# Seven-product FFN steps in another order, weight sums beside the down products, and the norm factor spread within the second product

## The chip, the core and the metric

The kernel runs on one core of one Trainium2 chip. The metric is the device time of one execution in microseconds, which holds the profiled span and about 1.8 us around it. Five engines work side by side, each through its own queue of instructions in a fixed order: TensorE (PE, matmuls), VectorE (DVE), ScalarE (ACT), GpSimd (POOL), and SyncE (SP), which here issues the DMAs.

## The reference, cut to what matters

```python
def _swiglu(h, w_up, w_down):
    a, g = jnp.split(h @ w_up, 2, axis=-1)
    return (jax.nn.silu(g) * a) @ w_down
...
x = x + 0.5 * _swiglu(_rmsnorm(x, g_ffn1), w_ffn1_up, w_ffn1_down)
x = x + mixer(_rmsnorm(x, g_mix), states)          # mLSTM and GLA side by side
x = x + 0.5 * _swiglu(_rmsnorm(x, g_ffn2), w_ffn2_up, w_ffn2_down)
y = _rmsnorm(x, g_final)
```

One decoder layer runs over 512 prompt and 64 sample tokens, 576 columns in all; the model is 1024 wide and the FFN 2816, so there are 22 tiles f of 128 FFN channels, each with a gate half and a value half. All is float32.

## The kernel before, in words

Activations lie transposed: eight tiles x0 to x7 of 128 channels by 576 tokens. Each float32 product is made of three matmuls, since weights and activations are split into a high and a low part (hi·hi, hi·lo, lo·hi). `whi` is a copy on ACT (`act`, L66), `wlo` a subtraction on DVE (`tt`, L54). Nearly all matmuls are 128x288, and 12 of them make one product of 1.60 us.

**Plain products.** `dense` (L130) and `mm3` (L114, matmul L122) compute a tile of 128 output channels against all eight input tiles in 48 matmuls. A function put on the list `midway` is called half way through the next such product. In FFN1 the first tile comes from `head` (L524, matmul L533), which takes the input tiles as they land. The RMS factor is not applied to the input: `Norm.square` sums the squares of x on POOL, `start` reduces them on TensorE and takes root and reciprocal, and `finish` (L247, matmuls L255) spreads the factor r over the partitions with eight small matmuls and two copies on ACT. The products are scaled by r as they leave PSUM: `G` at the mixer's start, `t` at an FFN's start.

**Seven-product steps.** The tiles f = 2 to 21 of each FFN use a scheme with seven products in place of eight. `Norm.combine` (L213) prepares the input combinations T1 to T4 (`xth`, `xtl`), `sums` (L368) the weight combinations: S1 and S2 on DVE, S3 and S4 on POOL, 128x512 each. A step runs seven products of 12 matmuls in the order NAMES (L308), A11, S2, A12, S3, S1, A22, S4. Then come two down products of an earlier group of tiles, named d0 and d1 here. For f = 2 to 5 these have 12 matmuls each, and a step is nine blocks of 1.60 us, 14.4 us. From f = 6 on they have 24, and a step is 17.6 us; there are 16 such steps in each FFN, of which the last two have one down product each and leave the rest behind them.

The order of all this is written by hand, and the scheduler keeps it (`tc.manual_schedule`, L435). `blocks` lists products and downs. `prep` and `prep_lo` make the weight parts of a block four blocks ahead. The sums for a step's weights are issued five blocks (S1, S2), four (S3) and two (S4) ahead of its A11. `later(d, fn)` issues `fn` d ticks on, where a product or half of a long down is one tick: `seven` (L389) uses it for s1, U2, U3, t and h, which join the products, and `done` (L457) for adding a down product to x (`stt`, L57).

PSUM sets the waits. The tag `pd` has two buffers. One holds A11 and A12 in one half, S1 and S4 in the other, and each down takes one as well, in turn. So d1 uses the buffer of the step's own pair, and the next step's A11 uses that of d0: it waits until x has taken d0 out. The tag `pm` (four banks) holds S2, S3 and A22. A12 adds to A11's bank after `s1` has copied it out, and S4 adds to that of S1 after `h` has read it.

The final norm works on half widths: `square` adds seven of eight squares up on POOL and hands the last, unadded, to the sum on TensorE (`packed_sum`, L150, matmul L156).

Of the kernel before, what the change touches and what calls it, by code (L numbers as in the profile page):

```python
# [9 lines left out]
F32 = mybir.dt.float32  # L10
# [18 lines left out]
GRP = 4  # L29
NH = 4  # L30
# [7 lines left out]
def step_kernel(ctx: ExitStack, tc: tile.TileContext, a):  # L38
# [125 lines left out]
    class Norm:  # L164
# [48 lines left out]
        def combine(self, q, pool):  # L213
# [33 lines left out]
        def finish(self, keep=True):  # L247
# [3 lines left out]
            r = xs.tile([P, 4 * n], F32, name="r", tag="r", bufs=1) if keep else None  # L251
# [10 lines left out]
    def ffn(x, norm, wup, wdn, fp, after, head=None, parts=((0, 1),)):  # L262

# [13 lines left out]
        for f in range(PLAIN):  # L277
# [30 lines left out]
        NAMES = ("A11", "S2", "A12", "S3", "S1", "A22", "S4")  # L308
        XOF = {"A11": "B11", "S2": "T2", "A12": "B21", "S3": "T3", "S1": "T1", "A22": "T4", "S4": "B22"}
        first = [0] + list(range(PLAIN, NF, GRP))  # L310
        size = [PLAIN] + [GRP] * (len(first) - 1)
        blocks, at_f = [], {}
        for g in range(1, len(first)):
            last = g == len(first) - 1
            o = 0
            for j in range(size[g]):
                f = first[g] + j
                at_f[f] = len(blocks)
                blocks += [(f, n) for n in NAMES]
# [6 lines left out]
        raw, parts_of, posts = {}, {}, {}  # L326
        pair = [None]
        tick = [0]

        def prep(i):  # L330

            b = blocks[i]
            if i % 2 == 0:
                pair[0] = [wp.tile([P, KT, P], F32R, name=f"w{n}", tag=f"w{n}", bufs=3) for n in ("hi", "lo")]
            if b[0] == "d":
                n = size[b[1]]
                src = raw["d"][b[1:]]
            else:
                n = 4
                src = raw[b[0]][b[1]]  # L340
            hi, lo = (t[:, 4 * (i % 2):4 * (i % 2) + n, :] for t in pair[0])
            act(hi, src, AF.Copy)
            parts_of[i] = hi, lo, src

        def prep_lo(i):
            hi, lo, src = parts_of[i]
            tt(lo, src, hi, ALU.subtract)
            parts_of[i] = hi, lo

        def load_up(f):  # L350
            st = wp.tile([P, 2, 4, P], F32, name="wst", tag="wst", bufs=3)
            su = fp.tile([P, 2, 4, P], F32, name="wsu", tag="wsu", bufs=2)
            for i, t in ((1, su), (0, st)):
                nc.sync.dma_start(out=t, in_=wup[f, :, i].rearrange("p (h k) c -> p h k c", h=2))
            raw[f] = {"A11": st[:, 0], "A12": st[:, 1], "A21": su[:, 0], "A22": su[:, 1]}

        def load_down(i):

            raw.setdefault("d", {})
            st = wp.tile([P, KT, P], F32, name="wst", tag="wst", bufs=3)  # L360
            _, g, o, hfs = blocks[i]
            n = size[g]
            sv_ = st[:, :2 * n, :].rearrange("p (o k) c -> p o k c", o=2)
            nc.sync.dma_start(out=sv_, in_=wdn[o:o + 2, :, first[g]:first[g] + n].rearrange("o p k c -> p o k c"))
            for u in range(2):
                raw["d"][(g, o + u, hfs)] = sv_[:, u]

        def sums(f, *names):  # L368
            w = raw[f]
            for n in names:  # L370
                a, b, op, eng = {"S1": ("A21", "A22", ALU.add, None), "S2": ("S1", "A11", ALU.subtract, None),
                                 "S3": ("A11", "A21", ALU.subtract, nc.gpsimd),
                                 "S4": ("A12", "S2", ALU.subtract, nc.gpsimd)}[n]
                w[n] = fp.tile([P, 4, P], F32, name=n, tag=n, bufs=1)
                tt(w[n], w[a], w[b], op, eng=eng)

        events = {}

        def on(i, fn, *a_):
            events.setdefault(i, []).append((fn, a_))  # L380

        for f, i in at_f.items():
            on(i - 11, load_up, f)
# [12 lines left out]
        def seven(f, psum, lastf):
# [3 lines left out]
            s1, U2, U3 = (fp.tile([P, HALF], F32, name=n, tag=n, bufs=1) for n in ("s1", "U2", "U3"))  # L400
            t1, t2, h1, h2, r2 = t[:, :HALF], t[:, HALF:], h[:, :HALF], h[:, HALF:], r[:, HALF:]
# [18 lines left out]
        def run(i, work):  # L420

            for m in work:
                nc.tensor.matmul(m[0], lhsT=m[1], rhs=m[2], start=m[3], stop=m[4], skip_group_check=m[5])  # L423
            do = events.pop(i, ())
            for fn, a_ in do:
                if fn is prep:
                    fn(*a_)
            for fn in posts.pop(tick[0], ()):
                fn()
            for fn, a_ in do:  # L430
                if fn is not prep:
                    fn(*a_)
            tick[0] += 1

        with tc.manual_schedule():  # L435
            for i in range(min(events), 0):
                for fn, a_ in events.pop(i, ()):
                    fn(*a_)
            psum = {}
            for i, b in enumerate(blocks):  # L440
                if b[0] == "d":
                    _, g, o, hfs = b
                    n = size[g]
                    hi, lo = parts_of.pop(i)
                    ps = pd.tile([P, 2, 512], F32, name="pd", tag="pd")
                    work = [(ps[:, hf, :HALF], wt[:, k, :], xt[:, hf * HALF:(hf + 1) * HALF],
                             k == 0 and m == 0, k == n - 1 and m == 2, False)
                            for k in range(n) for m, (wt, xt) in enumerate(
                                ((hi, mids[g][k][0]), (hi, mids[g][k][1]), (lo, mids[g][k][0]))) for hf in hfs]
                    half = 12 if len(work) > 12 else len(work)  # L450
                    run(i, work[:half])
                    if midway:
                        midway.pop()()
                    if work[half:]:
                        run(i, work[half:])

                    def done(ps=ps, o=o, hfs=hfs, fin=g == len(first) - 1):  # L457
                        s_ = slice(hfs[0], hfs[-1] + 1)
                        stt(halves(x[o])[:, s_], ps[:, s_, :HALF], 0.5, ALU.mult, halves(x[o])[:, s_], ALU.add)
                        if fin:  # L460
                            later(1, lambda: after(o, hfs))
# [883 lines left out]
```

## Time and profile before

| | |
|---|---|
| median of 3 runs (lowest to highest) | 1604.41 us (1603.92 to 1604.53) |
| profiled execution: its time, its span | 1603.93 us, 1602.1 us |
| busy: PE, DVE, ACT, POOL | 1563.5 us (98%), 1061.5 (66%), 678.4 (42%), 310.0 (19%) |
| 128x288 matmuls of the down products, mean length | 296 ns, one starting every 133 ns |

TensorE is busy nearly throughout. Lengths of matmuls overlap, so its progress is read from one start to the next. A line of the timeline gives in brackets how long the engine sat idle before the instruction, and what released it.

### The profile page before, as it was taken

How to read it: one execution, taken by the hardware profiler on the slowest of the kernel's cores; microseconds unless marked ns; L12 is line 12 of the kernel's file. 1: busy time of each engine (PE TensorE's matmuls, PEld its weight loads, DVE VectorE, ACT ScalarE, POOL GpSimd, SP SyncE). 2: the span in 40 equal slices, each digit the busy share in tenths (PEclk: the TensorE clock that was granted, in tenths of full speed). 3: DMA queues.
4: the chain of work that ended last, by engine and by line, in shares of the span. 5: the costliest groups of instructions: out<-in, count | busy, mean ns of one | idle time of the engine just before them, and what ended most of it. 6: DMA issues, size and time to landing. Idle time of an engine off the chain costs nothing.

```text
span 1602.1 us, 31170 instructions
## 1 busy us (share of the span) xinstructions
PE 1563.5 (98%) x13028; PEld 1514.5 (95%) x13028; DVE 1061.5 (66%) x1785; ACT 678.4 (42%) x1147; POOL 310.0 (19%) x300
## 2 busy tenths in 40 slices
PE   8999999999999999999999999999999999999997
PEld 7999999999998989999998989999999999999997
DVE  7986776767587666653565756633567977677775
ACT  8433433333555453631334344531453433333334
POOL 1333223321200000000100001003223422322223
PEclk9999999999999999999999999999999999999999
DMA  5222332233513313323432334442222232223223
GB/s 188 82 96 80 94 93 91 80 92 95 189 54 123 110 48 116 112 94 114 129 136 90 132 108 153 152 158 79 80 93 66 83 102 93 79 81 105 93 66 112
DMA packets 59332, 166.01 MB, mean 104 GB/s; under 512 B 6072, under 2 KB 14008, under 8 KB 58168
## 3 DMA queue, kind: packets, MB, share of 16 engines
q1 hardware_dynamic: 58616, 163.43, 31.8%
q8 instruction: 103, 1.69, 0.4%
q10 hardware_dynamic: 576, 0.59, 0.1%
q14 instruction: 37, 0.30, 0.1%
HBM read 142.60 MB, written 21.38 MB: 102 GB/s over the span
## 4 chain that ended last, share of the span: by engine, by line
PE 87%; DVE 6%; ACT 3%; issue 2%; POOL 1%; DMA 0%; SPq 0%; ACTq 0%; DVEq 0%; POOLq 0%
PE pd L122 36%; PE pd L423 32%; PE pm L423 10%; ACT whi L66 1%; DVE wlo L54 1%; PE pm L1075 1%; PE pm L794 1%; PE pd L533 1%; PE pm L1089 1%; PE pm L869 1%; DVE xt L57 1%; DVE ml L54 1%; PE pm L1141 1%; PE pm L722 1%; DVE xtl L54 0%
## 5 line engine op out<-in xcount | busy, mean ns | idle before, releaser
L66 ACT ACTIVATE whi<-wst 128x512 fp32r<-128x512 f32 (+3 forms) x301 | 217.9, 736 | 448.0 <-PE pd L122 271.8
L54 DVE TENSOR_TENSOR wlo<-wst,whi 128x512 fp32r<-128x512 f32 (+3 forms) x301 | 262.0, 871 | 22.4 <-ACT whi L66 15.1
L122 PE MATMUL pd<-xh,whi 128*128 128x288 f32 x1136 | 249.2, 298 | 5.4 <-DVE t L54 3.5
L122 PE MATMUL pd<-xh,wlo 128*128 128x288 f32 x1136 | 247.6, 296 | 0.0
L122 PE MATMUL pd<-xl,whi 128*128 128x288 f32 x1136 | 247.4, 297 | 0.0
L122 PEld LDWEIGHTS pd<-xh,whi 128*128 128x128 f32 x1136 | 182.8, 188 | 10.4 <-issue 9.7
L54 POOL TENSOR_TENSOR t<-t,r 128x288 f32<-128x288 f32 (+1 forms) x80 | 105.2, 1315 | 445.6 <-DVE t L54 399.6
L66 ACT ACTIVATE whi<-S 128x512 fp32r<-128x512 f32 x160 | 99.7, 626 | 208.9 <-PE pd L423 74.8
L122 PEld LDWEIGHTS pd<-xh,wlo 128*128 128x128 f32 x1136 | 183.5, 189 | 1.9 <-issue 1.8
L122 PEld LDWEIGHTS pd<-xl,whi 128*128 128x128 f32 x1136 | 182.6, 188 | 1.4 <-issue 1.0
L57 DVE SCALAR_TENSOR_TENSOR x<-pd,x 128x576 f32<-128x576 f32 (+1 forms) x112 | 79.8, 713 | 142.9 <-PE pd L423 116.8
L423 PE MATMUL pd<-mh,whi 128*128 128x288 f32 x704 | 156.3, 296 | 0.3 <-DVE x L57 0.3
L423 PE MATMUL pd<-mh,wlo 128*128 128x288 f32 x704 | 155.9, 296 | 0.0
L423 PE MATMUL pd<-ml,whi 128*128 128x288 f32 x704 | 155.9, 296 | 0.0
L423 PE MATMUL pd<-xh,whi 128*128 128x288 f32 x480 | 144.4, 301 | 7.5 <-DVE h L54 3.0
L423 PE MATMUL pm<-xth,wlo 128*128 128x288 f32 x480 | 141.9, 296 | 0.9 <-DVE wlo L54 0.9
L423 PE MATMUL pd<-xh,wlo 128*128 128x288 f32 x480 | 142.4, 297 | 0.0
L423 PE MATMUL pd<-xl,whi 128*128 128x288 f32 x480 | 142.3, 296 | 0.0
L423 PE MATMUL pm<-xth,whi 128*128 128x288 f32 x480 | 141.9, 296 | 0.0
L423 PE MATMUL pm<-xtl,whi 128*128 128x288 f32 x480 | 141.8, 296 | 0.0
L54 DVE TENSOR_TENSOR wlo<-S,whi 128x512 fp32r<-128x512 f32 x160 | 126.5, 791 | 0.6
L423 PEld LDWEIGHTS pd<-mh,whi 128*128 128x128 f32 x704 | 114.9, 189 | 0.7 <-DVE x L57 0.5
(318 smaller groups left out, 3227.9 us busy)
## 6 DMA issues: line engine op xcount, KB each, us to landing
wst<-in_win SPq DMA_DIRECT2D x65, 512.0 KB, 3.7
wst<-in_wup SPq DMA_DIRECT2D x46, 512.0 KB, 4.8
wst<-in_wdn SPq DMA_DIRECT2D x44, 512.0 KB, 3.7
wsu<-in_wup SPq DMA_DIRECT2D x40, 512.0 KB, 4.0
C<-in_C SPq DMA_DIRECT2D x16, 514.0 KB, 5.0
out_Cs<-C SPq DMA_DIRECT2D x16, 514.0 KB, 3.1
S<-in_S SPq DMA_DIRECT2D x4, 1024.0 KB, 4.9
out_Ss<-S SPq DMA_DIRECT2D x4, 1024.0 KB, 4.1
```

What stands on the lines that cost most here:

```text
L54: (eng or nc.vector).tensor_tensor(out=out, in0=in0, in1=in1, op=op)
L57: nc.vector.scalar_tensor_tensor(out=out, in0=in0, scalar=s, in1=in1, op0=op0, op1=op1)
L66: nc.scalar.activation(out=out, in_=in_, func=func, **kw)
L122: nc.tensor.matmul(ps[:, hf, :HALF], lhsT=wt[:, k, :], rhs=xt[:, hf * HALF:(hf + 1) * HALF], start=(k == 0 and n == 0), stop=(k == nk - 1 ...
L423: nc.tensor.matmul(m[0], lhsT=m[1], rhs=m[2], start=m[3], stop=m[4], skip_group_check=m[5])
L533: nc.tensor.matmul(ps[i][:, hf, :HALF], lhsT=wt[:, k, :], rhs=xt[:, hf * HALF:(hf + 1) * HALF], start=(k == 0 and n == 0), stop=(k == KT - ...
L722: nc.tensor.transpose(out=pt[:, c, j * P:(j + 1) * P], in_=src[j][:, (c0 + c) * P:(c0 + c + 1) * P], identity=ident)
L794: nc.tensor.matmul(po[32 * g:32 * g + 32, :], lhsT=qpad(b_)[j], rhs=states(b_)[j], start=(v == 0 and j == 0), stop=False)
L869: nc.tensor.matmul(pl[32 * g:32 * g + 32, c, :], lhsT=kk[:, o:o + 32], rhs=qq[:, o:o + 32], start=True, stop=True)
L1075: nc.tensor.matmul(pc, lhsT=ktok[:, c, j * P:(j + 1) * P], rhs=vtok[:, c, :], start=True, stop=True)
L1089: nc.tensor.matmul(po[:, c, :], lhsT=Cc[c - 1][:, d, es], rhs=qs[d][:, c * P:(c + 1) * P], start=False, stop=(d == 1))
L1141: nc.tensor.matmul(pu, lhsT=kb[:, b_ // 4, b_ % 4, j * P:(j + 1) * P], rhs=vb[:, b_ // 4, :], start=True, stop=True)
```

## The change

The order of the seven products becomes A11, A22, S2, S3, S1, A12, S4, and the functions that join them move with it. Weight parts are made three blocks ahead (LEAD). S1, S2 and S3 of a step are formed two blocks ahead of it, behind the first of the two downs, and S4 in the tick of A11. Down weights move from the buffers `wst` to `wsu`, which become three. At the start of the mixer and of FFN2 `finish` is called half way through the second plain product; before, it came after that product. `midway` is now taken from its front. At the program's head x0 is loaded behind 128 KB of weights; before, behind 256 KB. In the final norm the last two squares go to TensorE unadded, so each half has one POOL addition less and four small matmuls more. `combine` issues its last two operations in the other order.

```diff
+LEAD = 3
-                midway.pop()()
+                midway.pop(0)()
         def square(self, k, s=slice(0, T)):
+            last = KT - 1 if n == T else KT - 2
-            if k == 0 or k == KT - 1:
+            if k == 0 or k >= last:
                 acc.append(sq)
         def combine(self, q, pool):
+            stt(v[:, 1], c[:, :HALF], g, ALU.mult, u[:, 1], ALU.subtract)
             stt(v[:, 0], c[:, HALF:], g, ALU.mult, b[:, HALF:], ALU.subtract)
-            stt(v[:, 1], c[:, :HALF], g, ALU.mult, u[:, 1], ALU.subtract)
...
-        NAMES = ("A11", "S2", "A12", "S3", "S1", "A22", "S4")
+    NAMES = ("A11", "A22", "S2", "S3", "S1", "A12", "S4")
...
-            later(2, lambda: tt(U2, psum["S2"], s1, ALU.add))
-            later(3, lambda: tt(t1, psum["A11"], r[:, :HALF], ALU.mult))
-            later(6, lambda: tt(h1, psum["A22"], U3, ALU.add))
+        later(3, lambda: tt(U2, psum["S2"], s1, ALU.add))
+        later(6, lambda: tt(t[:, :HALF], psum["A11"], r[:, :HALF], ALU.mult))
+        later(6, lambda: tt(h[:, :HALF], psum["A22"], U3, ALU.add))
...
-            su = fp.tile([P, 2, 4, P], F32, name="wsu", tag="wsu", bufs=2)
+            su = fp.tile([P, 2, 4, P], F32, name="wsu", tag="wsu", bufs=3)
         def load_down(i):
-            st = wp.tile([P, KT, P], F32, name="wst", tag="wst", bufs=3)
+            st = fp.tile([P, KT, P], F32, name="wsu", tag="wsu", bufs=3)
...
-            on(i - 5, sums, f, "S1", "S2")
-            on(i - 4, sums, f, "S3")
-            on(i - 2, sums, f, "S4")
+                on(i - 2 if down else i - 3, sums, b[0], "S1", "S2")
+                on(i - 2 if down else i - 3, sums, b[0], "S3")
+                on(i, sums, b[0], "S4")
-            on(i - 4, prep, i)
-            on(i - 4, prep_lo, i)
+            on(i - LEAD, prep, i)
+            on(i - LEAD, prep_lo, i)
...
-            later(e[2], lambda: tt(h, h, t, ALU.mult))
-            later(e[3], lambda: tt(lo, h, hi, ALU.subtract))
+            later(e[2], lambda: tt(h, h, t, ALU.mult), not lastf)
+            later(e[3], lambda: tt(lo, h, hi, ALU.subtract), not lastf)
...
     def ffn(x, norm, wup, wdn, fp, after, head=None, parts=((0, 1),)):
                 pg = up(f, 0)
+                if f == 0:
+                    midway.append(norm.finish)
                 pa = up(f, 1)
                 if f == 0:
-                    r = norm.finish()
+                    r = norm.r
...
-        load_w(0, 2)
-        load(0, 1)
-        load_w(2, 5)
+        load_w(0, 1)
+        load(0)
+        load_w(1, 3)
+        load(1)
+        load_w(3, 5)
...
         midway.append(n2.start)
-        first = [win_tile(), win_tile()]
-        r = n2.finish()
+        first = [win_tile()]
+        midway.append(n2.finish)
+        first.append(win_tile())
+        r = n2.r
```

The third argument of `later` puts a function behind the tick's `wlo` subtraction. The block list, the loads and the loop around them are moved into a function `pipeline`, with no other change in what they issue.

VectorE, end of a step in the first group (f = 2). `wlo` are low weight parts, `S1` and `S2` weight sums, `t` and `h` the joins, and `x0` the addition of d0 to x, for which the next step's A11 waits. Before, from U3 to x0:

```order
L54 TENSOR_TENSOR U3_544<-pm_596,U2_543 128x288
L54 TENSOR_TENSOR S1_628<-wsu_528 128x512
L54 TENSOR_TENSOR S2_630<-S1_628,wst_527 128x512
L54 TENSOR_TENSOR wlo_625<-wst_537,whi_624 128x256
L54 TENSOR_TENSOR h_541<-pd_539,U3_544 128x288
L54 TENSOR_TENSOR wlo_625<-wst_527,whi_624 128x512
L54 TENSOR_TENSOR h_541<-pm_633,U3_544 128x288
L54 TENSOR_TENSOR wlo_664<-S2_630,whi_663 128x512
L54 TENSOR_TENSOR t_540<-pd_539,U2_543 128x288
L54 TENSOR_TENSOR wlo_664<-wst_527,whi_663 128x512
L57 SCALAR_TENSOR_TENSOR x0_83<-pd_668,x0_83 128x576
```

Now, from the first half of t to x0:

```order
L55 TENSOR_TENSOR t_542<-pd_541,r_330 128x288
L55 TENSOR_TENSOR h_543<-pm_565,U3_548 128x288
L55 TENSOR_TENSOR wlo_644<-wst_529,whi_643 128x512
L55 TENSOR_TENSOR t_542<-pd_541,U2_547 128x288
L55 TENSOR_TENSOR wlo_678<-wsu_530,whi_677 128x512
L55 TENSOR_TENSOR S1_687<-wsu_530 128x512
L55 TENSOR_TENSOR S2_689<-S1_687,wst_529 128x512
L58 SCALAR_TENSOR_TENSOR x0_83<-pd_664,x0_83 128x576
```

The two sums have moved from behind U3 to between the second half of t and x0.

VectorE at the start of FFN2, where `t` takes the first gate product out of PSUM; `wlo` (128x1024) belongs to the fourth plain product, `xtl` to the input combinations. Before:

```order
L57 SCALAR_TENSOR_TENSOR xt_13661<-x7_11968,sm_72,xt_13660 128x288
L54 TENSOR_TENSOR wlo_13737<-wst_13735,whi_13736 128x1024
L54 TENSOR_TENSOR xtl_13659<-xt_13660,xth_13658 128x576
L54 TENSOR_TENSOR xtl_13659<-xt_13661,xth_13658 128x576
L54 TENSOR_TENSOR t_13670<-pd_13489,r_13605 128x576
```

Now:

```order
L58 SCALAR_TENSOR_TENSOR xt_13667<-x7_11974,sm_72,xt_13666 128x288
L55 TENSOR_TENSOR xtl_13665<-xt_13666,xth_13664 128x576
L55 TENSOR_TENSOR t_13676<-pd_13495,r_13587 128x576
L55 TENSOR_TENSOR xtl_13665<-xt_13667,xth_13664 128x576
L55 TENSOR_TENSOR wlo_13743<-wst_13741,whi_13742 128x1024
```

`t` stands ahead of that `wlo` and of the last `xtl`.

## Rows read from the trace of the kernel before

**Rows 1.** The page, part 4: shares of the chain that ended last, by engine.

```profile
PE 87%; DVE 6%; ACT 3%; issue 2%; POOL 1%; DMA 0%; SPq 0%; ACTq 0%; DVEq 0%; POOLq 0%
```

**Rows 2.** TensorE's waits: what waited, the releaser: us in total, times, longest.

```profile
PE pd L423 <- DVE h L54: 3.0, 4, 1.3
PE pd L423 <- ACT whi L66: 2.9, 4, 0.8
PE pd L423 <- DVE t L54: 2.0, 13, 0.2
```

**Rows 3.** Stages: length; PE, PEld, DVE, ACT, POOL busy; clock; DMA share; GB/s.

```profile
0.00:26.00 26.00, 19.41 (x163) 16.97 (x164) 17.11 (x27) 20.95 (x34) 1.81 (x6) 1.00 0.83 279
41.00:52.00 11.00, 8.72 (x52) 8.26 (x52) 10.12 (x15) 4.32 (x9) 2.71 (x2) 0.84 0.22 72
1184.00:1217.00 33.00, 29.51 (x223) 28.94 (x222) 24.72 (x40) 19.11 (x29) 7.73 (x5) 0.95 0.10 34
```

**Rows 4.** Timeline (start us, length us), TensorE, twice the wait of full steps.

```profile
146.81 0.40 PE L423 MATMUL pd<-xth,whi 128*128 128x288 f32 x1 [0.15 <-DVE t L54]
...
182.45 0.40 PE L423 MATMUL pd<-xth,whi 128*128 128x288 f32 x1 [0.15 <-DVE t L54]
```

**Rows 5.** Timeline, TensorE, two waits in the first group of FFN1.

```profile
83.81 0.37 PE L423 MATMUL pd<-xh,whi 128*128 128x288 f32 x1 [0.83 <-ACT whi L66]
...
114.51 0.37 PE L423 MATMUL pd<-xh,whi 128*128 128x288 f32 x1 [1.30 <-DVE h L54]
```

**Rows 6.** Timeline, VectorE then GpSimd, end of a step in that group.

```profile
86.03 0.68 DVE L54 TENSOR_TENSOR wlo<-wst,whi 128x512 fp32r<-128x512 f32 x1
...
87.25 0.76 DVE L57 SCALAR_TENSOR_TENSOR x<-pd,x 128x576 f32<-128x576 f32 x1 [0.54 <-PE pd L423]
...
90.98 1.74 DVE L54 TENSOR_TENSOR wlo<-wsu,whi 128x512 fp32r<-128x512 f32 x1
...
87.34 1.29 POOL L54 TENSOR_TENSOR S<-wst,S 128x512 f32<-128x512 f32 x1
...
90.43 1.74 POOL L54 TENSOR_TENSOR S<-wst,wsu 128x512 f32<-128x512 f32 x1
```

**Rows 7.** Timeline, TensorE then VectorE, start of FFN1's seven products.

```profile
42.70 0.40 PE L423 MATMUL pm<-xth,wlo 128*128 128x288 f32 x1 [0.92 <-DVE wlo L54]
...
45.65 0.48 PE L423 MATMUL pd<-xh,whi 128*128 128x288 f32 x1 [1.35 <-ACT s L66]
...
49.27 0.29 PE L423 MATMUL pm<-xth,whi 128*128 128x288 f32 x1
...
38.98 1.83 DVE L54 TENSOR_TENSOR h<-raw,t 128x576 f32<-128x576 f32 x1 [1.33 <-POOL t L54]
...
40.73 1.91 DVE L54 TENSOR_TENSOR wlo<-S,whi 128x512 fp32r<-128x512 f32 x1
```

**Rows 8.** Timeline, TensorE then VectorE, start of the mixer.

```profile
433.00 0.50 PE L122 MATMUL pd<-xh,whi 128*128 128x288 f32 x2 [1.92 <-DVE G L54]
...
420.89 1.05 DVE L245 RECIPROCAL v<-v 128x144 f32<-128x144 f32 x1 [1.51 <-ACT v L66]
```

**Rows 9.** Timeline, TensorE then VectorE, start of FFN2.

```profile
1202.42 0.50 PE L122 MATMUL pd<-xh,whi 128*128 128x288 f32 x2 [3.49 <-DVE t L54]
...
1199.06 1.21 DVE L54 TENSOR_TENSOR wlo<-wst,whi 128x1024 fp32r<-128x1024 f32 x1
1200.19 1.41 DVE L54 TENSOR_TENSOR xtl<-xt,xth 128x576 fp32r<-128x576 f32 x2
1201.53 0.74 DVE L54 TENSOR_TENSOR t<-pd,r 128x576 f32<-128x576 f32 x1
```

**Rows 10.** Timeline, GpSimd then TensorE, the final norm.

```profile
1592.02 0.79 POOL L54 TENSOR_TENSOR acc<-acc,sq 128x288 f32<-128x288 f32 x1
...
1592.86 0.36 PE L156 MATMUL pm<-acc,cst 128*32 128x72 f32 x8 [2.05 <-POOL acc L54]
```

**Rows 11.** Timeline, TensorE, the first matmuls of the program.

```profile
6.58 1.09 PE L533 MATMUL pd<-xh,whi 128*128 128x288 f32 x3 [6.58 <-ACT xh L66]
```

More of the change, by code (lines that the diff above doesn't have):

```diff
@@ L250, in finish @@
             per = 2 if n == T // 4 else 4
-            r = xs.tile([P, 4 * n], F32, name="r", tag="r", bufs=1) if keep else None
+            self.r = r = xs.tile([P, 4 * n], F32, name="r", tag="r", bufs=1) if keep else None
             for i in range(4 // per):
@@ L260, in finish, with unite @@
             return r
+    NAMES = ("A11", "A22", "S2", "S3", "S1", "A12", "S4")
+    XOF = {"A11": "B11", "S2": "T2", "A12": "B21", "S3": "T3", "S1": "T1", "A22": "T4", "S4": "B22"}
+    def unite(psum, t, h, r, fp, later):
+        s1, U2, U3 = (fp.tile([P, HALF], F32, name=n, tag=n, bufs=1) for n in ("s1", "U2", "U3"))
+        later(1, lambda: act(s1, psum["A11"], AF.Copy))
+        later(3, lambda: tt(U2, psum["S2"], s1, ALU.add))
+        later(4, lambda: tt(U3, psum["S3"], U2, ALU.add))
+        later(5, lambda: tt(h[:, HALF:], psum["S1"], U3, ALU.add))
+        later(6, lambda: tt(t[:, :HALF], psum["A11"], r[:, :HALF], ALU.mult))
+        later(6, lambda: tt(h[:, :HALF], psum["A22"], U3, ALU.add))
+        later(7, lambda: tt(t[:, HALF:], psum["S1"], U2, ALU.add))
@@ L304, in ffn @@
             mids[0].append((hi, lo))
-        NAMES = ("A11", "S2", "A12", "S3", "S1", "A22", "S4")
-        XOF = {"A11": "B11", "S2": "T2", "A12": "B21", "S3": "T3", "S1": "T1", "A22": "T4", "S4": "B22"}
         first = [0] + list(range(PLAIN, NF, GRP))
         size = [PLAIN] + [GRP] * (len(first) - 1)
-        blocks, at_f = [], {}
+        blocks = []
         for g in range(1, len(first)):
@@ L316, in ffn @@
             for j in range(size[g]):
-                f = first[g] + j
-                at_f[f] = len(blocks)
-                blocks += [(f, n) for n in NAMES]
+                blocks += [(first[g] + j, n) for n in NAMES]
                 for _ in range(1 if last and j >= GRP - 2 else 2):
@@ L324, in ffn @@
         blocks += [("d", len(first) - 1, o, hfs) for hfs in parts for o in range(KT)]
[L326 to L351, printed above, removed]
-            su = fp.tile([P, 2, 4, P], F32, name="wsu", tag="wsu", bufs=2)
-            for i, t in ((1, su), (0, st)):
-                nc.sync.dma_start(out=t, in_=wup[f, :, i].rearrange("p (h k) c -> p h k c", h=2))
-            raw[f] = {"A11": st[:, 0], "A12": st[:, 1], "A21": su[:, 0], "A22": su[:, 1]}
@@ L357, in load_down @@
-        def load_down(i):
-            raw.setdefault("d", {})
-            st = wp.tile([P, KT, P], F32, name="wst", tag="wst", bufs=3)
[L361 to L383, printed above, removed]
-            on(i - 5, sums, f, "S1", "S2")
-            on(i - 4, sums, f, "S3")
-            on(i - 2, sums, f, "S4")
-        for i, b in enumerate(blocks):
-            if b[0] == "d" and b[2] % 2 == 0:
-                on(i - 8, load_down, i)
-            on(i - 4, prep, i)
-            on(i - 4, prep_lo, i)
-        def later(d, fn):
-            posts.setdefault(tick[0] + d, []).append(fn)
@@ L396, in seven, with up_done @@
-        def seven(f, psum, lastf):
+        def up_done(f, psum, later):
+            if (f - PLAIN) % GRP == 0:
+                mids.append([])
             t = fp.tile([P, T], F32, name="t", tag="t", bufs=2)
             h = fp.tile([P, T], F32, name="h", tag="h", bufs=2)
-            s1, U2, U3 = (fp.tile([P, HALF], F32, name=n, tag=n, bufs=1) for n in ("s1", "U2", "U3"))
-            t1, t2, h1, h2, r2 = t[:, :HALF], t[:, HALF:], h[:, :HALF], h[:, HALF:], r[:, HALF:]
+            lastf = f == NF - 1
@@ L413, in seven @@
-            later(7, lambda: tt(t2, t2, r2, ALU.mult, eng=pool_))
+            unite(psum, t, h, r, fp, later)
+            later(7, lambda: tt(t[:, HALF:], t[:, HALF:], r[:, HALF:], ALU.mult, eng=pool_))
             later(e[0], lambda: act(t, t, AF.Silu))
             later(e[1], lambda: tt(t, t, r, ALU.mult, eng=pool_))
-            later(e[2], lambda: tt(h, h, t, ALU.mult))
+            later(e[2], lambda: tt(h, h, t, ALU.mult), not lastf)
             later(e[3], lambda: act(hi, h, AF.Copy))
-            later(e[3], lambda: tt(lo, h, hi, ALU.subtract))
@@ L420, in run @@
[L420 to L461, printed above, removed]
-                    later(0, done)
-                    continue
-                f, n = b
-                if n == "A11":
-                    if (f - PLAIN) % GRP == 0:
-                        mids.append([])
-                    pair_ = pd.tile([P, 2, 512], F32, name="pd", tag="pd")
-                    psum = {"A11": pair_[:, 0, :HALF], "S1": pair_[:, 1, :HALF]}
-                    psum["A12"], psum["S4"] = psum["A11"], psum["S1"]
-                    seven(f, psum, f == NF - 1)
-                if n not in psum:
-                    psum[n] = bank([P, HALF], "b" + n)
-                hi, lo = parts_of.pop(i)
-                go_on = n in ("A12", "S4")
-                run(i, [(psum[n], wt[:, k, :], xt, not go_on and k == 0 and m == 0, k == 3 and m == 2, go_on)
-                        for k, (xh, xl) in enumerate(norm.block(XOF[n]))
-                        for m, (wt, xt) in enumerate(((hi, xh), (hi, xl), (lo, xh)))])
-            while posts:
-                for fn in posts.pop(min(posts)):
-                    fn()
@@ new lines, in up_done, with down_work @@
+            later(e[3], lambda: tt(lo, h, hi, ALU.subtract), not lastf)
+        def down_work(b, w, ps):
+            _, g, o, hfs = b
+            n = size[g]
+            hi, lo = w
+            return [(ps[:, hf, :HALF], wt[:, k, :], xt[:, hf * HALF:(hf + 1) * HALF],
+                     k == 0 and m == 0, k == n - 1 and m == 2, False)
+                    for k in range(n) for m, (wt, xt) in enumerate(
+                        ((hi, mids[g][k][0]), (hi, mids[g][k][1]), (lo, mids[g][k][0]))) for hf in hfs]
@@ new lines, in down_done @@
+        def down_done(b, ps, later):
+            _, g, o, hfs = b
+            s_ = slice(hfs[0], hfs[-1] + 1)
+            stt(halves(x[o])[:, s_], ps[:, s_, :HALF], 0.5, ALU.mult, halves(x[o])[:, s_], ALU.add)
+            if g == len(first) - 1:
+                later(1, lambda: after(o, hfs))
+        pipeline(blocks, norm, fp, lambda f, i: wup[f, :, i], up_done,
+                 (lambda b: size[b[1]], lambda b: wdn[b[2]:b[2] + 2, :, first[b[1]]:first[b[1]] + size[b[1]]],
+                  down_work, down_done))
```

114 lines of the change are left out of this document (110 added, 4 removed).

## The prediction

> **What bounds the kernel.** I read the page first. TensorE has 87% of the chain that ended last and VectorE 6% [rows 1]. So the kernel can only get shorter by the time in which TensorE stands still, or runs at half clock. I then read TensorE's waits [rows 2], the stages' clocks [rows 3], and the timeline at each wait. There the reader is to see three kinds. In the long steps one small wait of 0.15 us comes back [rows 4]. In the first and last groups a few larger ones stand [rows 2, 5]. And there are the starts, where VectorE is late by 1 to 3.5 us and the clock falls behind it in two places [rows 3, 7 to 9]. Fewer matmuls are not on offer: the change removes none and adds eight small ones. The sum is made against the profiled execution, 1603.93 us, which lies 0.5 under the median of 1604.41.
>
> **Long steps.** TensorE waits 13 times for `t` [rows 2]: S1 shares the buffer of A11 and A12, and the old order reads t out of it before S1 may start. From one such start to the next lie two steps, 264 matmuls or 35.2 us. They took 182.45 - 146.81 = 35.64 [rows 4], so a pair loses 0.44, the restart included. There are seven starts of this kind in each FFN, by their spacing 14 in all, one of them too short to be listed. In the new order S1 writes into the other half five products after the pair's buffer was freed, and t is read only after A12. That removes 14 x 0.43 = **6.0**. What is late next? `h` must have read S1 before S4 starts. S1 ends 8.0 us into the step and S4 starts at 9.6; a join has half the width of x0's 0.76 [rows 6] and takes about 0.5, so 1.1 us are spare. `x0` now stands behind two sums, but a long d1 gives it 3.2 us, and 2.4 are spare. Both are covered while VectorE keeps within these.
>
> **Last groups.** The waits for `whi` and `h` come four times each, 5.9 us in all [rows 2]. The two of the first group, 0.83 and 1.30 [rows 5], come in both FFNs and make 4.3, so 1.6 belong to the last groups. With a restart of 0.2 each that is 2.4. In the old order A12 comes third and waits for weights and for the copy of A11; it now comes sixth. I take **2.4** as gained.
>
> **First groups.** This is the loss. A12's waits go here too, but a new one comes. Of the old waits: between the two rows of [rows 5] lie two steps of 14.4; they took 30.70, so 1.9 were lost. The earlier pair loses 0.83 and about 0.7 around it, which makes 3.4 per FFN. In the new order the next A11 needs the PSUM buffer of d0, so it needs x0, and x0 stands on VectorE behind t, `wlo`, S1 and S2. Count from the end of S4's product: d0 and d1 take 3.2. VectorE needs 0.4 for the half t, three times about 0.65 (a 128x512 operation alone is 0.68, its queue overlapping a little), and 0.76 for x0 [rows 6], some 3.1. It would just do. But GpSimd does the half product t*r and the sum S3 in the same 3 us. A 128x512 subtraction beside such a sum took 1.74 in place of 0.68 and ended 0.55 after GpSimd's operation [rows 6]. So one collision costs 1.06 and two 2.1. I take 1.4, one in full and a part of the shorter one, at the four steps that follow (f = 3 to 6): 5.6 against 3.4, a loss of 2.2 per FFN, **-4.4**. The ends are 0 per boundary (+6.8) and 2.1 (-10.0).
>
> Why such an operation ends when GpSimd's does: the Trainium skill, SBUF — State Buffer, section "SBUF: two separate sides", says that VectorE with two SBUF inputs and GpSimd share a port pair under an exclusive lock, and that whichever starts first keeps it for the whole instruction. The 0.55 agrees with that. By this rule alone both GpSimd operations, 0.79 for a half width and 1.29 for the sum [rows 6, 10], would shut VectorE out one after the other. The boundary would then cost 2.1, and my sum would end 5.6 later, at 1595.8. The row shows one collision and its 1.06, not a second one.
>
> **FFN1's start.** Now TensorE waits 0.92 for `wlo` and 1.35 for the copy `s` [rows 7]. It then runs at half clock: 15 matmuls from 45.65 to 49.27 take 3.62 in place of 2.0, the clock granted in that stage is 0.84 [rows 3]. With the restarts all that costs 4.2. The cause is VectorE: `h` had to wait for GpSimd's t and then took 1.83, and the `wlo` behind it 1.91 [rows 7]. Without the sum S3 between the two t, `h` still ends near 41.0. Then S2's sum and A22's `wlo` follow, each 0.65, and A22 has its low part at 42.3, where it wants it 0.7 earlier. S2's `wlo` comes behind ml and h and costs some 0.45. Two waits under 0.8 should not lower the clock, since one of 1.30 [rows 5] didn't. So 1.1 remain: **+3.1**, between 1 and 4.2.
>
> **Mixer's start.** TensorE stands 1.92 because `G` waits for r, and r is spread only after the second tile [rows 8]. The root's reciprocal was done at 420.89 + 1.05, so the spread may run half way through that tile, near 427. It removes the wait and its restart: **+2.0**, between 1.0 and 2.1. The eight small matmuls only change places.
>
> **FFN2's start.** TensorE stands 3.49 [rows 9], then runs at 240 ns per matmul for 15 of them, which is 1.6 more; the stage shows 0.95 of the clock [rows 3]. Here r is not the last thing: VectorE works without a pause and issues `t` behind a `wlo` of 1.21 and two `xtl` [rows 9]. Now `t` stands ahead of that `wlo` and of one `xtl`, so it starts at about 1199.7 and ends at 1200.4. TensorE, free since 1202.42 - 3.49 = 1198.93, waits 1.6. That `wlo` belongs to the fourth product, 6.4 us off, which covers it. A wait of 1.6 I take to leave the clock full, as 1.92 did at the mixer. Gained: 1.9 + 1.6 = **+3.5**, between 1.9 and 5.1.
>
> **Ends.** The final sum waits 2.05 for GpSimd's additions [rows 10]. One of 0.79 on the path goes, four small matmuls come: **+0.8** (0 to 0.9). At the head TensorE starts at 6.58 when x0 has landed [rows 11]. 128 KB less stand before it; at 279 GB/s [rows 3] that is 0.46. SyncE issues one pair of loads more ahead of x1 and x2, so I keep **+0.3** (0 to 0.9). LEAD, the new buffers and the order in `combine` I cost at nothing: a part made three blocks ahead still has 4.8 us for 1.3 us of work.
>
> **Sum.** 6.0 + 2.4 - 4.4 + 3.1 + 2.0 + 3.5 + 0.8 + 0.3 = 13.7, and 1603.93 - 13.7 = **1590.2 us**.
>
> **Rivals.** (a) *The boundary hides.* VectorE's three operations get in before GpSimd's, and x0 is ready on time. For it: alone they take 3.1 of 3.2. Against it: t*r starts as soon as t is done, just when they do. With a wait of 0.6 the term becomes +2.0, with none +6.8: 1579 to 1584. (b) *VectorE is the bound at the starts.* Its work there isn't less, only in another order, and it runs without pause [rows 9]. If FFN1's and FFN2's starts give back what they gain, 6.6 go, if the mixer's does too, 8.6: 1597 to 1599. (c) *Slower: the joins fall behind in every long step.* `h` has 1.1 us before S4, and `wlo` and `ml` stand ahead of it on VectorE. Were two of them stretched to 1.74 [rows 6], 2.1 would be added and S4 would wait 1.0, in 32 steps: 1622. It decides from a lag of 1.1, and from 1.1 + 0.43 on (13.7 / 32) the whole gain is gone. Against it: in long steps GpSimd is free for most of the time. (d) *The spread doesn't move*, because the engines' queues keep it late, and the starts stay as they are while the rest of the sum is eaten by the boundary at 2.1: 1601 to 1604. The order of the instructions speaks against it.
>
> **How the numbers follow.** The forecast has 0.52 (its own range 1586 to 1595), (a) 0.22, (b) 0.15, (c) 0.06, (d) 0.05. The range takes in the forecast, most of (a) and (b): 1581 to 1599. A measurement of this kernel can tell 0.2%, 3.2 us, from no change. Faster than 1601.2: 0.52 + 0.22 + 0.14 = 0.88. Slower than 1607.6: 0.06. The same: 0.06.
>
> **What would show it.** The 13 waits for `t` are gone. At f = 3 to 6 the first matmul of a step waits for `x`, by 1 to 2 us. The first matmul after the spread at 1199 waits about 1.6 and stages 41 to 52 and 1184 to 1217 show the full clock. `G`'s wait is gone. I am wrong if waits for `h` or `x` stand in the long steps, if the boundaries show nothing or more than 2.1, or if the starts keep their half clock.

## The result, and the profile after

The changed kernel takes 1647.88 us (median of 6 runs, 1646.84 to 1650.64) against 1604.16 for the kernel before: a ratio of 1.0276 with an interval of 1.0263 to 1.0290. It is slower by 44 us where I had forecast 14 less, and lies far above the range.

The page of the changed kernel, parts 1 and 4 (busy time with its share, then the chain):

```profile
PE 1577.1 (96%) x13044; PEld 1524.2 (92%) x13044; DVE 1150.6 (70%) x1787; ACT 673.1 (41%) x1149; POOL 330.3 (20%) x298
...
PE 87%; DVE 7%; ACT 3%; issue 2%; POOL 1%; DMA 0%; SPq 0%; DVEq 0%; ACTq 0%; POOLq 0%
```

The chain is spread as before [rows 1], so it tells nothing here. TensorE's waits do (us in total, times, longest):

```profile
PE pd L358 <- ACT whi L67: 22.2, 24, 2.3
PE pd L358 <- DVE h L55: 12.8, 20, 0.6
PE pd L358 <- DVE x L58: 9.3, 4, 2.3
...
PE pd L358 <- DVE t L55: 3.0, 8, 0.4
PE pm L358 <- DVE wlo L55: 1.8, 2, 1.2
PE pd L123 <- DVE t L55: 1.7, 1, 1.7
```

The 13 small waits for `t` before S1 [rows 2] are gone, and the wait for `G` of [rows 8] too; the eight for `t` that are listed now stand before the second down of the short steps. New are 44 waits for `h` and `whi` and four for `x`. Eight of these 48, four named `x` and four of those named `whi`, are step boundaries of the first groups, 2.33 each. The other 40 are 0.64 each: 20 named `h` make 12.8, and 20 named `whi` make the 22.2 less 4 x 2.33. There are 40 steps in the two FFNs, so every step has one. This is what it looks like in a long step; first TensorE, then VectorE:

```profile
163.11 0.29 PE L358 MATMUL pd<-xth,whi 128*128 128x288 f32 x1
...
164.69 0.29 PE L358 MATMUL pd<-xh,whi 128*128 128x288 f32 x1
...
166.16 0.29 PE L358 MATMUL pd<-xh,wlo 128*128 128x288 f32 x1
167.09 0.37 PE L358 MATMUL pd<-xh,whi 128*128 128x288 f32 x1 [0.64 <-ACT whi L67]
```

```profile
164.34 0.68 DVE L55 TENSOR_TENSOR wlo<-wsu,whi 128x512 fp32r<-128x512 f32 x1
166.49 0.46 DVE L55 TENSOR_TENSOR h<-pd,U 128x288 f32<-128x288 f32 x1 [1.47 <-PE pd L358]
...
168.95 0.46 DVE L55 TENSOR_TENSOR t<-pd,r 128x288 f32<-128x288 f32 x1 [1.41 <-PE pd L358]
...
170.29 0.45 DVE L55 TENSOR_TENSOR t<-pd,U 128x288 f32<-128x288 f32 x1
```

S1 runs from 163.11, A12 from 164.69 (last matmul at 166.16), S4 from 167.09. `h` reads only S1's half of the PSUM tile, which was complete by 164.9. Yet VectorE stood idle for 1.47 and took `h` at 166.49, when A12 had ended. S4 must wait for `h`, hence the 0.64; with the restart it is 0.88, since 166.16 to 167.09 is 0.93 in place of 0.13 and the next start is 0.08 late. In the same way `t`, which reads A11 and A12's half, started only at 168.95, when S4 had ended. That VectorE is idle before both speaks against my rival (c), where it had too much to do.

In the first group the same delay meets the sums. VectorE, GpSimd and TensorE at one boundary:

```profile
73.93 0.46 DVE L55 TENSOR_TENSOR t<-pd,r 128x288 f32<-128x288 f32 x1 [1.69 <-PE pd L358]
...
76.24 1.30 DVE L55 TENSOR_TENSOR S<-wsu 128x512 f32<-128x512 f32 x1
77.57 1.64 DVE L55 TENSOR_TENSOR S<-S,wst 128x512 f32<-128x512 f32 x1
79.13 0.74 DVE L58 SCALAR_TENSOR_TENSOR x<-pd,x 128x576 f32<-128x576 f32 x1
```

```profile
75.80 1.18 POOL L55 TENSOR_TENSOR t<-t,r 128x288 f32<-128x288 f32 x1 [11.48 <-DVE t L55]
76.94 1.71 POOL L55 TENSOR_TENSOR S<-wst,wsu 128x512 f32<-128x512 f32 x1
```

```profile
75.87 0.51 PE L358 MATMUL pd<-mh,whi 128*128 128x288 f32 x2 [0.38 <-DVE t L55]
...
80.02 0.37 PE L358 MATMUL pd<-xh,whi 128*128 128x288 f32 x1 [2.33 <-ACT whi L67]
...
80.92 0.45 PE L358 MATMUL pd<-xh,wlo 128*128 128x288 f32 x1
81.16 0.45 PE L358 MATMUL pd<-xh,whi 128*128 128x288 f32 x1
```

`t` comes late, so the second down waits for the buffer (0.38), VectorE's queue starts late, and both sums are stretched beside GpSimd. The next A11 waits 2.33, and what follows runs at 240 ns per matmul, half clock. Of the eight boundaries six are followed by 11 to 14 such matmuls, the last one in each FFN by none.

### The profile page after: what moved, and what is told of

It reads as the page before. It is cut to its first block, busy times and chain, and to the rows that moved or that the text cites. A ratio compares the mean times of both kernels' runs of the same rounds, so it can differ in the third digit from the quotient of the medians.

```text
span 1648.9 us, 31241 instructions
## 1 busy us (share of the span) xinstructions
PE 1577.1 (96%) x13044; PEld 1524.2 (92%) x13044; DVE 1150.6 (70%) x1787; ACT 673.1 (41%) x1149; POOL 330.3 (20%) x298
## 4 chain that ended last, share of the span: by engine, by line
PE 87%; DVE 7%; ACT 3%; issue 2%; POOL 1%; DMA 0%; SPq 0%; DVEq 0%; ACTq 0%; POOLq 0%
PE pd L123 35%; PE pd L358 31%; PE pm L358 12%; DVE S L55 1%; ACT whi L67 1%; DVE wlo L55 1%; DVE h L55 1%; PE pd L566 1%; PE pm L1110 1%; PE pm L829 1%; PE pm L1124 1%; PE pm L904 1%; DVE xt L58 1%; PE pm L1176 1%; PE pm L757 0%
## 5 line engine op out<-in xcount | busy, mean ns | idle before, releaser
L67 ACT ACTIVATE whi<-wst 128x1024 fp32r<-128x1024 f32 (+3 forms) x199 | 160.0, 806 | 297.9 <-PE pd L123 264.1
L67 ACT ACTIVATE whi<-S 128x512 fp32r<-128x512 f32 x160 | 95.5, 621 | 310.9 <-DVE S L55 295.1
L55 DVE TENSOR_TENSOR wlo<-wst,whi 128x1024 fp32r<-128x1024 f32 (+3 forms) x199 | 184.0, 926 | 14.3 <-ACT whi L67 10.2
L358 PE MATMUL pd<-xh,whi 128*128 128x288 f32 x480 | 148.3, 309 | 44.5 <-ACT whi L67 22.2
L123 PEld LDWEIGHTS pd<-xh,whi 128*128 128x128 f32 x1136 | 182.8, 188 | 6.8 <-issue 4.1
L55 DVE TENSOR_TENSOR wlo<-S,whi 128x512 fp32r<-128x512 f32 x160 | 178.2, 1133 | 3.4 <-ACT whi L67 0.8
L358 PEld LDWEIGHTS pd<-xh,whi 128*128 128x128 f32 x480 | 92.1, 192 | 54.9 <-ACT whi L67 37.3
```

The lines of the kernel that those rows point to most:

```text
L55: (eng or nc.vector).tensor_tensor(out=out, in0=in0, in1=in1, op=op)
L67: nc.scalar.activation(out=out, in_=in_, func=func, **kw)
L123: nc.tensor.matmul(ps[:, hf, :HALF], lhsT=wt[:, k, :], rhs=xt[:, hf * HALF:(hf + 1) * HALF], start=(k == 0 and n == 0), stop=(k == nk - 1 ...
```

## The experiments

Three theories stood at first. T1: a PSUM tile is waited for as a whole, so a read of one half waits for the last matmul issued into the other. T2: VectorE and GpSimd are overfull where the sums now stand. T3: three blocks are too short for the weight parts.

**S1 and S4 in a PSUM tile of their own** (called the own-bank kernel):

```diff
-                    psum = {"A11": pair_[:, 0, :HALF], "S1": pair_[:, 1, :HALF]}
-                    psum["A12"], psum["S4"] = psum["A11"], psum["S1"]
+                    psum = {"A11": pair_[:, 0, :HALF], "A12": pair_[:, 0, :HALF]}
...
-                    psum[n] = bank([P, HALF], "b" + n)
+                    psum[n] = psum["S1"] if n == "S4" else bank([P, HALF], "b" + n)
```

> The changed kernel, but S1 and S4 go into a PSUM bank of their own (tag pm) in place of the second half of the tile that A11 and A12 use. Theory T1 (a PSUM tile is waited for as a whole: h, reading S1's half, waits for the end of A12, which the new order puts between them, and t, reading A12's half, for the end of S4): the wait of 0.64 before S4 is gone in all 40 steps, about 35 us with restarts, the wait of the second down in the first groups too, and their boundary shrinks by the 1.6 us that t and h start earlier; 1588 to 1602 us. Theory T2 (VectorE and GpSimd are overfull where the sums now stand, and the joins are late for that): h still starts late, 1635 to 1648. Theory T3 (three blocks are too short for the weight parts; the page names ScalarE's whi for most of the wait): 1640 to 1650.

Measured: 1592.17 us (1591.88 to 1594.35), 0.9937 of the kernel before (0.9923 to 0.9952): 55.7 less than the changed kernel. VectorE in a long step, and TensorE at a boundary of the first group:

```profile
150.46 0.46 DVE L55 TENSOR_TENSOR h<-pm,U 128x288 f32<-128x288 f32 x1 [0.52 <-PE pm L358]
...
152.06 0.46 DVE L55 TENSOR_TENSOR t<-pd,r 128x288 f32<-128x288 f32 x1 [0.54 <-PE pd L358]
```

```profile
74.81 0.37 PE L358 MATMUL pd<-xh,whi 128*128 128x288 f32 x1 [1.62 <-ACT whi L67]
```

A12 starts at 150.26 and S4 at 151.85 here. `h` is taken at S1's end, `t` at A12's, and no wait is left in the long steps. T1 holds. The boundary fell from 2.33 to 1.62. The name must not mislead: the two halves lay in separate banks before, 512 float32 apart in one tile, and what the edit gives S1 and S4 is a tile of their own.

The program tells the same. TensorE's matmuls raise a count, and other engines wait until it has reached a number (`waits PE_49`). In VectorE's queue the second half of `t`, which needs S4, has no wait of its own in the changed kernel (the first three rows), since the first half has already waited for S4. In the own-bank kernel (the last three) it has one. For `h` out of S1 in the same step the number is 408 in the changed kernel, reached by A12's last matmul, and 396 in the own-bank kernel, reached by S1's last; the 12 between are A12's. So the wait is put into the program when the kernel is built. Whether the chip itself would need it, no run asked.

```
L55 TENSOR_TENSOR t_712<-pd_711,r_330 128x288 [waits PE_49]
L55 TENSOR_TENSOR h_713<-pm_740,U3_718 128x288
...
L55 TENSOR_TENSOR t_712<-pd_711,U2_717 128x288

L55 TENSOR_TENSOR t_713<-pd_712,r_330 128x288 [waits PE_49]
L55 TENSOR_TENSOR h_714<-pm_741,U3_719 128x288
...
L55 TENSOR_TENSOR t_713<-pm_791,U2_718 128x288 [waits PE_49]
```

**The old order in the changed kernel:**

```diff
-    NAMES = ("A11", "A22", "S2", "S3", "S1", "A12", "S4")
+    NAMES = ("A11", "S2", "A12", "S3", "S1", "A22", "S4")
...
-        later(3, lambda: tt(U2, psum["S2"], s1, ALU.add))
+        later(2, lambda: tt(U2, psum["S2"], s1, ALU.add))
-        later(6, lambda: tt(t[:, :HALF], psum["A11"], r[:, :HALF], ALU.mult))
+        later(3, lambda: tt(t[:, :HALF], psum["A11"], r[:, :HALF], ALU.mult))
...
-                on(i - 2 if down else i - 3, sums, b[0], "S1", "S2")
+                on(i - 3, sums, b[0], "S1", "S2")
```

> The changed kernel with the order of the products and the ticks of the joins as before (S1 and S2's sums one block earlier, since S2 is the second product again); weight sums, lead, buffers, spread and head stay changed. T1: the long steps have only the small wait for t again, 1592 to 1606. T2 and T3: most of the loss stays, 1625 to 1648.

Measured: 1583.45 us (1582.93 to 1583.83), ratio 0.9881 (0.9864 to 0.9897). With the old order, and S1 and S2's sums one block earlier, the whole loss is gone. What is left of TensorE's waits in the seven-product steps:

```profile
PE pd L358 <- DVE x L58: 2.3, 8, 0.3
PE pm L358 <- DVE wlo L55: 1.8, 1, 1.8
```

It is even faster than T1 gave. The small waits for `t` before S1 did not come back, nor did those for `whi` and `h` in the first and last groups [rows 2]; that VectorE is in time because the sums are out of its way is my reading and not shown by itself. Here A22, which has a bank of its own, stands between S1 and S4, and `h` waits for nothing but S1.

**The new order alone, in the kernel before:**

```diff
-        NAMES = ("A11", "S2", "A12", "S3", "S1", "A22", "S4")
+        NAMES = ("A11", "A22", "S2", "S3", "S1", "A12", "S4")
...
-            later(2, lambda: tt(U2, psum["S2"], s1, ALU.add))
-            later(3, lambda: tt(t1, psum["A11"], r[:, :HALF], ALU.mult))
+            later(3, lambda: tt(U2, psum["S2"], s1, ALU.add))
...
+            later(6, lambda: tt(t1, psum["A11"], r[:, :HALF], ALU.mult))
             later(6, lambda: tt(h1, psum["A22"], U3, ALU.add))
```

> The kernel before with nothing changed but the order of the seven products and the ticks of the joins; sums five, four and two blocks ahead, lead four, as before. T1: every step waits 0.64 before S4, 0.88 with the restart, 40 times 35 us, less the waits that go (about 10): 1622 to 1640. T2: no loss without the moved sums, 1590 to 1606. T3: no loss, 1590 to 1606.

Measured: 1625.83 us (1625.02 to 1626.60), ratio 1.0144 (1.0129 to 1.0160), in T1's range and far outside the others'. Its waits:

```profile
PE pd L423 <- DVE h L54: 18.1, 23, 1.5
PE pd L423 <- ACT whi L66: 11.0, 17, 0.7
```

Again 40, one per step, most of 0.64 and some longer in the first group. With lead four and the sums at their old place T2 and T3 have nothing left to explain them.

**The sums at their old places in the changed kernel:**

```diff
-                on(i - 2 if down else i - 3, sums, b[0], "S1", "S2")
-                on(i - 2 if down else i - 3, sums, b[0], "S3")
-                on(i, sums, b[0], "S4")
+                on(i - 5, sums, b[0], "S1", "S2")
+                on(i - 4, sums, b[0], "S3")
+                on(i - 2, sums, b[0], "S4")
```

> The changed kernel with the weight sums back at five, four and two blocks ahead. T1: the long steps keep their wait before S4 (28 us in 32 steps), only the boundaries of the first groups gain, 1620 to 1640. T2: the loss goes, 1590 to 1606. T3: nothing goes, 1642 to 1650.

Measured: 1617.38 us (1616.83 to 1618.05), ratio 1.0092 (1.0077 to 1.0107): 30 less than the changed kernel, a little more than T1's 8 to 28. The 40 waits stay; the eight boundaries go and the half clock behind them too (granted clock 1.00 between 51 and 131, 0.94 in the changed kernel):

```profile
PE pd L358 <- ACT whi L67: 13.6, 21, 0.7
PE pd L358 <- DVE h L55: 12.4, 19, 0.9
```

So the sums' place is a second cost, which counts only in the first groups.

**`h` issued ahead of A12**, one number in the changed kernel:

```diff
-        later(5, lambda: tt(h[:, HALF:], psum["S1"], U3, ALU.add))
+        later(4, lambda: tt(h[:, HALF:], psum["S1"], U3, ALU.add))
```

> The changed kernel with one number changed: the join h is issued before A12's matmuls in place of behind them. T1 (the tile is waited for as a whole, by the order of issue): h now starts at S1's end, but A12, which writes the other half, waits for h in place of S4: the wait of 0.64 moves from S4 to A12 and the time stays near the changed kernel's, 1632 to 1652. Rival (only the half that is read counts): h is done while A12 runs, no wait is left, 1605 to 1618.

Measured: 1648.72 us (1648.11 to 1651.36), ratio 1.0288 (1.0272 to 1.0303). VectorE and TensorE:

```profile
166.80 0.46 DVE L55 TENSOR_TENSOR h<-pd,U 128x288 f32<-128x288 f32 x1 [0.46 <-PE pd L358]
```

```profile
167.41 0.37 PE L358 MATMUL pd<-xh,whi 128*128 128x288 f32 x1 [0.64 <-DVE h L55]
```

In this place TensorE's next product is A12, and it waits the same 0.64, now because it writes into a tile of which the other half is still to be read. Issue order decides who waits; while both products lie in one tile, somebody does.

The rest concerns the other terms. **The spread alone**, in the kernel before:

```diff
                 pg = up(f, 0)
+                if f == 0:
+                    midway.append(norm.finish)
                 pa = up(f, 1)
...
-        first = [win_tile(), win_tile()]
-        r = n2.finish()
+        first = [win_tile()]
+        midway.append(n2.finish)
+        first.append(win_tile())
+        r = n2.r
```

> The kernel before with nothing changed but the norm factor's spread, half way through the second plain product at the mixer and at FFN2. The prediction's two terms: 2.0 and 3.5, together 5.5 under the kernel before, 1596 to 1600 us beside some 1602 to 1604. Rival (VectorE is the bound at FFN2's start): only the mixer's 2.0, 1600 to 1602.

Measured: 1598.16 us (1595.58 to 1598.80), ratio 0.9973 (0.9962 to 0.9984), which is 2.6 to 6.1 us and holds the 5.5; the medians, 1602.13 for the kernel before beside it, lie 4.0 apart. The wait at FFN2's start:

```profile
1198.36 0.53 PE L122 MATMUL pd<-xh,whi 128*128 128x288 f32 x2 [1.41 <-DVE t L54]
```

It is 1.41 in place of 3.49 [rows 9], near the 1.6 worked out, and what follows runs at full clock.

**Own bank, with S3 a block later:**

```diff
-                on(i - 2 if down else i - 3, sums, b[0], "S3")
+                on(i - 1, sums, b[0], "S3")
```

> The own-bank kernel with GpSimd's sum S3 one block later, behind the second down in place of the first, so that it does not run beside VectorE's S1 and S2. If GpSimd's operation shuts VectorE out (1.06 in the kernel before), the boundary falls from 1.62 to about 0.6 and the time by 8 us: 1581 to 1587. Rival (VectorE's queue is too long by itself): the boundary stays over 1.3, 1589 to 1594.

Measured: 1592.65 us (1592.27 to 1593.51), boundary 1.62. It tells nothing: GpSimd has nothing else queued there, and took S3 at the same point, right behind t*r, as in the own-bank kernel. An issue place moves an operation only if something stands between.

**Own bank, without S3's sum:**

```diff
             for n in names:
+                if n == "S3":
+                    w[n] = w["A11"]
+                    continue
```

> The own-bank kernel without GpSimd's sum S3: the product S3 takes the weights A11 unsummed, which leaves out 40 additions of 128x512 on GpSimd and nothing else. If GpSimd's operation shuts VectorE out: S2's sum falls from 1.66 to 0.69, the boundary from 1.62 to about 0.65, the time by 8 times 0.97 to 1583 to 1586 us. Rival (VectorE's queue is too long by itself): boundary over 1.3, 1589 to 1594.

Measured: 1584.13 us (1584.05 to 1584.18), ratio 0.9882 (0.9865 to 0.9898); it leaves the sum S3 out, so its output is not the layer's. VectorE's two sums, then TensorE at the boundary:

```profile
69.18 1.30 DVE L55 TENSOR_TENSOR S<-wsu 128x512 f32<-128x512 f32 x1
70.51 0.69 DVE L55 TENSOR_TENSOR S<-S,wst 128x512 f32<-128x512 f32 x1
```

```profile
72.02 0.37 PE L361 MATMUL pd<-xh,whi 128*128 128x288 f32 x1 [0.66 <-ACT whi L67]
```

The second sum is back at 0.69, the first, beside t*r, still takes 1.30. Taking 40 additions from GpSimd, an engine with 20% to do, gave 8.0 us on TensorE.

**Own bank, VectorE's sums one block earlier**, as in the old-order kernel:

```diff
-                on(i - 2 if down else i - 3, sums, b[0], "S1", "S2")
+                on(i - 3, sums, b[0], "S1", "S2")
```

> The own-bank kernel with VectorE's sums S1 and S2 one block earlier, ahead of the second half of t, where GpSimd has nothing to do. By the port theory the boundary falls to 0.3 to 0.5, as in the old-order kernel, and the time to 1580 to 1585 us. Rival (queue too long): 1588 to 1593.

Measured: 1582.73 us (1582.10 to 1583.41), ratio 0.9873 (0.9858 to 0.9888), 1.3% under the kernel before. It is the lowest median of all, though its interval overlaps that of the old-order kernel. Both sums take 0.69 there, and the boundary is gone; what is left is

```profile
PE pm L358 <- DVE h L55: 3.6, 8, 0.5
```

a wait for `h` before S4 at f = 3 to 6 of each FFN, which I had not expected.

**Two with all sums at their old places**, in the own-bank kernel and in the old-order kernel (the edit shown above, with lead three):

> The changed kernel with S1 and S4 in a bank of their own, and with the weight sums back at five, four and two blocks ahead. In the own-bank kernel (1592.2 us) what is left in the first groups is a wait of 1.62 at eight step boundaries, 14 us with restarts. If the sums between t and x0 are its cause, it goes: 1576 to 1584. Rival (VectorE's work in a step of 14.4 us is too much wherever the sums stand): it moves to another wait, 1586 to 1594.

Measured: 1585.03 us (1584.31 to 1585.52), ratio 0.9892 (0.9877 to 0.9906). Between the two expectations: the boundaries are gone, but S4 waits 0.35 to 0.86 for `h` in the first groups.

> The changed kernel with the order of the products, the ticks of the joins and the places of the weight sums as before; lead three, buffers, spread, head and final norm stay changed. The old-order kernel (1583.5 us) has waits of 0.3 at eight boundaries and one of 1.8 at FFN1's start. If the sums before x0 cause the eight, 3.5 us go: 1578 to 1582. Rival (the old places bring back the old waits for h and whi in the first groups, 3.4 per FFN): 1586 to 1592.

Measured: 1585.67 us (1585.20 to 1586.20), ratio 0.9897 (0.9881 to 0.9914), 2.2 slower than with the sums at i - 3, though the two intervals overlap. The rival is right in kind: waits of 0.35 to 0.48 for `h` came back in place of those for `x`, though not the whole 3.4 per FFN.

## Why the prediction was wrong

**Where it failed: "Long steps".** I wrote that S1 ends 8.0 us into the step and S4 starts at 9.6, so `h` has 1.1 to spare. It has none. `h` is issued behind A12 and reads the tile into which A12 goes, so it starts when A12 ends, at 9.6, and S4 waits for it in full. The own-bank kernel, the new order alone and `h` ahead of A12 show this from three sides. The sign stood in my own first term: TensorE waited 13 times for `t` before S1 [rows 2, 4], though `t` reads one half of that tile and S1 writes the other. I named the shared buffer as the cause and then counted the new order as if the halves were apart.

**What it cost**, by starts in the changed kernel's trace, for each FFN: 16 long or last steps times 0.88, 14.1; in the first group 4 x 0.88 before S4, 4 x 0.62 before the second down, 4 x 2.56 at the boundary and about 40 matmuls at half clock, 107 ns over each: 3.5 + 2.5 + 10.2 + 4.2 = 20.4. Both FFNs: 69. The own-bank kernel has 4 x 1.85 per FFN left of it, 15 in all. The difference, 54, is nearly all of the 55.7 measured between the two kernels.

**The other terms** can be read once that is out of the way. The own-bank kernel's 1592.2 lies 2.0 from the forecast, but it is only 10.1 under the kernel before beside it (1602.31), where I had 13.7: some of that nearness is luck. The terms below come to about 9.

- *Long steps, the old wait* (6.0) and *last groups* (2.4): both are gone in the own-bank kernel.
- *First groups* (-4.4): the mechanism was right, the size low. A boundary is 1.62, 1.85 with its restart, where I took 1.4. That is 14.8 for eight against 11.2, and the term comes to -8.0. Both collisions count: the sum beside t*r takes 1.30, the one beside S3 1.66. Without S3 the boundary lost 0.96 of its 1.62, which is the 0.97 by which the second sum got shorter. By the rule of the Trainium skill (SBUF — State Buffer, "SBUF: two separate sides"), that the side which comes second is shut out for the whole instruction, I had 2.1. The trace agrees with that in kind: two collisions, 0.62 and 0.98 over the 0.68 that such an operation takes alone, 1.6 in all.
- *FFN1's start* (+3.1): the clock stays full, as I had it, but the second wait is 1.18, not 0.45 (the row below); the two waits are 1.82 where I had 1.15. By starts from 38 to 51 TensorE loses 2.3 there, 4.3 before, so the term is some 2.0.
- *Mixer's and FFN2's start* (5.5): borne out. From FFN1's last down product to FFN2's first seven-product matmul the spread-alone kernel takes 794.6 us against 800.5 before, 5.9 less in these two executions; the medians differ by 4.0.
- *Ends* (+1.1): the head has its 0.5, the first matmul starting at 6.07 in place of 6.58 [rows 11]. At the end the sum waits 0.56 in place of 2.05 [rows 10], and 16 small matmuls came, not the eight that I counted (13044 in all against 13028). In the own-bank kernel the last down matmul starts 11.1 before the end, 11.6 in the kernel before: 0.5 of the 0.8 I had. In the changed kernel the eight matmuls of the last spread took 1.90, at half clock (granted 0.54 there), where the kernel before took 1.11 for them, and that ate the gain.

The changed kernel at the head, FFN1's start, FFN2's start and the end:

```profile
6.07 1.09 PE L566 MATMUL pd<-xh,whi 128*128 128x288 f32 x3 [6.07 <-ACT xh L67]
...
42.12 0.40 PE L358 MATMUL pm<-xth,wlo 128*128 128x288 f32 x1 [0.64 <-DVE wlo L55]
...
45.16 0.40 PE L358 MATMUL pm<-xth,wlo 128*128 128x288 f32 x1 [1.18 <-DVE wlo L55]
...
1223.84 0.54 PE L123 MATMUL pd<-xh,whi 128*128 128x288 f32 x2 [1.72 <-DVE t L55]
...
1640.32 1.90 PE L257 MATMUL pm<-v,cst 128*128 128x72 f32 x8 [1.05 <-DVE v L247]
```

Rival (c) had the place, S4 waiting for `h` in each step, and nearly the size, 1.0. Its mechanism, a VectorE that falls behind, was wrong, and so was the 0.06 I gave it: I argued against an overfull engine and did not ask what else `h` waits for.

## What to carry to other kernels

Dependencies here go by tile and by issue order, not by the part of a tile that is read. So when products are put in another order, write down for each reader of a shared PSUM tile the last write issued ahead of it, and count its start from the end of that one. A wait in the old trace that the data don't ask for (here `t` before S1) is the sign of such a rule; carry it over to the new order. Two products that are joined at different times want tiles of their own; separate banks within one tile were not enough here.

## What the runs showed that I had not expected

Where several releasers stand close together, the name in the waits view alternates: half of the 40 equal waits bear `whi`, half `h`, and `whi` (166.98 at its end, against 166.95 for `h`) is made three blocks ahead for another product. Only the experiment told them apart.

Half clock did not go by the length of the wait alone. A wait of 1.76 at FFN1's start of the old-order kernel was followed by 13 matmuls at 240 ns, and so was one of 1.35 behind one of 0.92 in the kernel before [rows 7]; 1.92 at the mixer's start [rows 8] and 1.72 at FFN2's start of the changed kernel were not. In the changed kernel 2.33 was, with waits of 0.64 and 0.38 ahead of it in the same step, at six boundaries of eight; at the other two, with the same waits, it wasn't. The old-order kernel (a matmul lasts 0.44 behind the wait), then a boundary of the changed kernel without half clock (0.29):

```profile
43.55 0.41 PE L358 MATMUL pm<-xth,wlo 128*128 128x288 f32 x1 [1.76 <-DVE wlo L55]
...
44.95 0.44 PE L358 MATMUL pm<-xth,wlo 128*128 128x288 f32 x1
```

```profile
119.81 0.37 PE L358 MATMUL pd<-xh,whi 128*128 128x288 f32 x1 [2.33 <-ACT whi L67]
...
120.95 0.29 PE L358 MATMUL pd<-xh,wlo 128*128 128x288 f32 x1
```

The first group's stage in the two kernels, changed and own-bank (length; PE, PEld, DVE, ACT, POOL busy; clock; DMA share; GB/s):

```profile
51.00:131.00 80.00, 65.96 (x442) 63.29 (x442) 62.55 (x86) 26.33 (x49) 23.82 (x16) 0.94 0.22 70
```

```profile
51.00:125.00 74.00, 67.51 (x504) 66.70 (x503) 68.84 (x96) 28.61 (x53) 27.97 (x19) 1.00 0.29 89
```

What exactly decides between the two levels was not tried.
